# A sixth kept weight unit, norm weights applied at the split, and plain fp32 for the early linear units of a two-layer trunk

## The chip, the cores and the metric

One Trainium2 chip, one of its cores. The metric is the device time of one execution in microseconds (us). Engines: PE (TensorE) does matmuls, ACT (ScalarE) and DVE (VectorE) element-wise work, POOL (GpSimd) a few small operations, SP (SyncE) issues the DMAs.

## What is computed

256 tokens of width 2048 pass through two layers. Layer 0 mixes tokens with a state-space model and a gated linear unit, layer 1 with latent attention; each is followed by a feed-forward layer. Around every sub-layer stand two RMS norms, with weights `norm_g[l, 0..3]`:

```python
h = rmsnorm(x, norm_g[l, 0])
m = s5_mixer(h, ...)            # layer 0; layer 1: mla_mixer(h, ...)
x = x + rmsnorm(m, norm_g[l, 1])
h = rmsnorm(x, norm_g[l, 2])
f = conv_ffn(h, w_gate[l], w_up[l], conv_w[l], conv_b[l], w_down[l])
x = x + rmsnorm(f, norm_g[l, 3])
```

`s5_mixer` ends in `val, gate = split(gelu(y) @ w_glu + b_glu)` and `val * sigmoid(gate)`; `w_glu` is 2048 x 4096. All of it is fp32.

## The kernel before, in words

Tokens lie on the 128 partitions in two blocks (`tb` 0 and 1). A weight unit is 1 MB, loaded by `wunit` (L76) into `raw` (two buffers). `split` (L72) cuts it in two: ACT copies a rounded high part (L73, fp32r), DVE subtracts it and leaves the remainder (L74). `mm3` (L107) then multiplies with three fp32r matmuls: high by high, high by remainder, remainder by high. A `raw` buffer is free when both halves are split. The activations are kept as such pairs too, transposed, in the tiles `act`.

The state-space stage (`s5`) runs 18 turns; in turn n it works on pieces n, n-1 and n-2 of sixteen. Small loads `bc` and `g` for the next piece are issued by SP (L415, L417). After each fourth piece `part_d` (L545) splits a quarter of the mixer's output, and four early linear units (`glu_early`, L243) join the list `todo`; each turn takes at most one from it. They make the first two of four column blocks of the value and of the gate, one quarter of the contraction at a time. `glu_rest` (L624) does what is left, then column blocks 2 and 3.

At the end of each sub-layer block 0's last column block comes first, so that its norms run while PE works on block 1. For this the last units of weights are kept (`held`), split into tiles of their own (slots of `HOLD5` and `HOLD`, L36 and L38): five units in `glu_rest`, four in the feed-forward layers and in attention. Block 0 uses each unit as it comes, block 1 uses all of them afterwards.

The chain of one block is then: `finish` (linear stage only, L625), `finish_chunk` (L163: ACT squares the chunk and sums, DVE multiplies by the norm weight on L166), `post_norm` (L168: reciprocal root with one POOL power, then four times the residual sum on L172, the squares on ACT, and on L178 the product with the next norm's weight), `pre_scale` (L180: a second reciprocal root and, on L182, a diagonal tile `xh`), `pre_turn` (L185: PE multiplies by that diagonal and so transposes and scales, L191; four 512-column splits follow). `done(tb, 0)` calls all but the turn, `done(tb, 1)` the turn. Block 1's turn is called by the next layer as `tail()`, behind that layer's first products for block 0, for which it too keeps its first four units (L737 in `ffn`, L858 in `attention`). Only the feed-forward layers use L178; attention puts its norm weight into its own weights (L100).

The framework orders each engine's instructions by a plan made when the kernel is built, from program order and estimated times; the chip then runs every queue in that order. So the next layer's splits may stand between the links of a chain.

Of the kernel before, what the change touches and what calls it, by code (L numbers as in the profile page):

```python
# [15 lines left out]
P = 128  # L16
# [19 lines left out]
HOLD5 = ((0, 2), (4, 6), (10, 12), (8, None), (None, None))  # L36
LATE = ((1, 1), (2, 1), (3, 1), (2, 0), (3, 0))
# [7 lines left out]
def tile_trunk(ctx: ExitStack, tc: tile.TileContext, a: dict):  # L45
# [84 lines left out]
    def gain_tile(src):  # L130
        return T(env["ap"], [P, D], F32, "gb", 2), src
# [36 lines left out]
    def post_norm(f, fst, tb, x, xst, g):  # L168
        r = rstd1(fst[tb], D)
        for n in range(NCH):  # L170
# [6 lines left out]
            if g is not None:  # L177
                dve.tensor_tensor(f[tb][:, c], x[tb][:, c], g[0][:, c], op=ALU.mult)  # L178

    def pre_scale(xst):  # L180
        d = T(env["ap"], [P, 512], F32, "xh", 2)[:, :P]
        dve.tensor_scalar(d, ident, rstd1(xst, D), None, op0=ALU.mult)  # L182
        return d

    def pre_turn(h, d, tb):  # L185
        for n in range(NCH):
# [5 lines left out]
            split(*acts4(tb, n, slice(0, 4)), ptv)  # L192
# [49 lines left out]

    def glu_early(f, n, b, half):  # L243
        hv = glu_load(n, b, half)
        banks = [accb(), accb()]
        for tb in range(NB):
            hk, u = hv
            for i, (wh, wl) in enumerate(u):
                for k in range(hk):
                    j = i * hk + k  # L250
                    mm3(banks[tb], *acts(tb, 4 * b + j), wh[:, k, :], wl[:, k, :], j == 0, j == 3)
        o = half * 1024 + n * 512
# [8 lines left out]
    def s5(f):  # L261
        with tc.tile_pool(name="s5", bufs=2) as q1:
# [277 lines left out]
            def glu_steps(b):  # L540
                for n in range(2):
                    for half in range(2):
                        yield glu_early(f, n, b, half)

            def part_d(qt, yg):  # L545
                act_tiles()
                for hh in range(2):
# [7 lines left out]
                    for tb in range(NB):  # L555
                        hi, lo = acts4(tb, qt, slice(0, 4))
                        split(av(hi), av(lo), ptv.rearrange("p t (j c) -> p t j c", j=4)[:, :, :, 16 * tb : 16 * tb + 16])
# [19 lines left out]
            for n in range(nb + 2):  # L577
# [14 lines left out]
                if n >= 2 and m % PB == PB - 1:  # L592
                    part_d(m // PB, yg)
                    todo.append(glu_steps(m // PB))
# [8 lines left out]
    gkv, gq = T(cp, [P, KT], F32, "gkv"), T(cp, [P, KT], F32, "gq")  # L603
    sync.dma_start(gkv, a["gkv"])
# [19 lines left out]
    def glu_rest(q1, todo, f, fst, gains, done):  # L624
        def finish(n, tb, banks, bb):  # L625
# [7 lines left out]
            finish_chunk(f, fst, tb, n, gains[0])  # L633
# [12 lines left out]
        for n in range(2, 4):  # L646
            banks = [(wk if n % 2 == 0 else accb)() for _ in range(4)]
            held = []
            for b in range(4):
                for half in range(2):  # L650
                    if n == 3 and (b, half) > (1, 0):
                        late = LATE[len(held)]
                        held.append((*late, glu_load(n, *late, HOLD5[len(held)])))
# [5 lines left out]
                if n == 2 and b < 2:  # L659
                    if b == 0:  # L660
                        gain_load(gains[0])
# [5 lines left out]
                if n == 3 and b == 0:  # L667
# [3 lines left out]
                    gain_load(gains[1])  # L671
                    bb = bias(n)
            pb = banks
        for tb in range(NB):
# [4 lines left out]
            finish(3, tb, banks, bb)  # L679
# [4 lines left out]
    def ffn(l, tail, gains, f, fst, done):  # L684
        with tc.tile_pool(name=f"ff{l}", bufs=2) as q1:
# [42 lines left out]
            for part, npair in enumerate(PARTS):  # L728
                hid = []
                for pr in range(p0, p0 + npair):  # L730
                    banks = [wk(), wk()] if pr == 0 else [[wk(), wk()] for _ in range(2)]
                    held = []
                    for which, w in enumerate((wg, wu)):
                        for kh in range(2):
                            v = w[:, 8 * kh : 8 * kh + 8, pr * S : (pr + 1) * S]
                            if pr == 0:
                                held.append((which, kh, wunit(v, 8, S, slots=HOLD[len(held)])))  # L737
# [37 lines left out]
                if part == len(PARTS) - 2:  # L775
                    for g in gains:
                        if g is not None:
                            gain_load(g)
# [5 lines left out]
                def evac(n, tb, bank):  # L784
# [5 lines left out]
                    if last:  # L790
                        finish_chunk(f, fst, tb, n, gains[0])
# [26 lines left out]
    def attention(tail, gains, f, fst, done):  # L818
        with tc.tile_pool(name="at", bufs=2) as q1:
# [34 lines left out]
            for which, (w, gain) in enumerate(((wdkv, gkv), (wdq, gq))):  # L854
                banks = [accb(), accb()]
                held = []
                for un in range(4):
                    hv = wunit(  # L858
                        w[:, 4 * un : 4 * un + 4, 0:RANK], 4, RANK, gain[:, 4 * un : 4 * un + 4],
                        slots=(None, None) if which else HOLD[un],  # L860
                    )
# [158 lines left out]
            for g in gains:  # L1020
                gain_load(g)
            for n in range(NCH):
                banks = [accb(), accb()] if n else wob
                held = []
                for un in range(0 if n else 3, 4):
                    if n < NCH - 1:
# [4 lines left out]
                for tb in range(NB):  # L1031
                    if tb:
                        for un, hv in enumerate(held):
                            down(banks[1], un, 1, hv)
                        if held:
                            done(0, 1)
                    c = f[tb][:, n * 512 : (n + 1) * 512]
                    act.activation(c, banks[tb], AF.Copy)
# [140 lines left out]
```

## Time and profile before

| | us |
|---|---|
| median of 3 runs (2193.27 to 2194.26) | 2193.63 |
| the profiled execution | 2187.58 |
| its span in the profile | 2185.8 |
| PE busy in the span | 2079.0 (95%) |
| DVE busy | 1408.8 (64%) |
| ACT busy | 1122.4 (51%) |
| POOL busy | 19.8 (1%) |

Busy time of PE includes matmuls that overlap; what counts at a border is the idle time that a row shows in brackets, and what ended it. An fp32 matmul leaves two records, an fp32r matmul one.

### The profile page before, as it was taken

What the parts mean: (1) busy time and instruction counts of PE and PEld (TensorE: products, weight loads), DVE (VectorE), ACT (ScalarE), POOL (GpSimd) and SP (SyncE); (2) the same over time, 40 slices, a digit from 0 to 9 for tenths busy, and PEclk for the clock granted to TensorE, in tenths of its full rate; (3) what the DMA queues carried; (4) which work ended last, traced back from release to release, by engine and by line L of the source; (5) the groups of instructions that cost most, each with busy time, mean ns of one, the idle gap of its engine ahead of it and who ended that gap; (6) DMA issues with size and microseconds to landing.
All of it is one profiled execution on the core that took longest, in us unless ns stands there. A gap on an engine that the chain in (4) does not pass through costs nothing.

```text
span 2185.8 us, 32404 instructions
## 1 busy us (share of the span) xinstructions
PE 2079.0 (95%) x13268; PEld 1764.2 (81%) x13268; DVE 1408.8 (64%) x1940; ACT 1122.4 (51%) x1695; POOL 19.8 (1%) x57
## 2 busy tenths in 40 slices
PE   3788999899999999999989999989999999999998
PEld 2566777888888888888878998788888888888886
DVE  7999666666466556655686665566646655665567
ACT  6677445455455445544464554545545544554444
POOL 0000000000000000000000000000000000000000
PEclk9999999999999999999999999999999999999999
DMA  4132476455565555555564434635555555555654
GB/s 131 50 98 75 154 233 206 145 188 179 193 197 187 193 193 191 178 190 193 192 200 129 136 118 155 212 123 189 189 193 193 180 187 193 193 183 184 194 191 154
DMA packets 280966, 374.74 MB, mean 171 GB/s; under 512 B 9200, under 2 KB 196208, under 8 KB 279792
## 3 DMA queue, kind: packets, MB, share of 16 engines
q1 hardware_dynamic: 280816, 372.66, 52.4%
q8 instruction: 104, 1.70, 0.3%
q14 instruction: 46, 0.38, 0.1%
HBM read 370.54 MB, written 2.10 MB: 170 GB/s over the span
## 4 chain that ended last, share of the span: by engine, by line
PE 82%; DVE 10%; DMA 4%; ACT 3%; issue 1%; POOL 0%; SPq 0%; DVEq 0%; POOLq 0%; ACTq 0%
PE wk L114 29%; PE wk L115 15%; PE acc L108 9%; PE acc L109 9%; PE acc L110 9%; DMA raw<-in_w_glu 3%; PE wk L108 2%; PE wk L109 2%; PE wk L110 2%; DVE wlo L74 2%; PE acc L191 1%; DVE x L74 1%; ACT whi L73 1%; DVE f L431 1%; DVE f L430 1%
## 5 line engine op out<-in xcount | busy, mean ns | idle before, releaser
L74 DVE TENSOR_TENSOR wlo<-raw,whi 128x1024 fp32r<-128x1024 f32 (+2 forms) x640 | 761.0, 1191 | 584.0 <-ACT whi L73 579.3
L73 ACT ACTIVATE whi<-raw 128x1024 fp32r<-128x1024 f32 (+2 forms) x640 | 658.3, 1031 | 635.3 <-PE wk L114 245.6
L114 PE MATMUL wk<-act,whi 128*128 128x512 f32 x2688 | 941.9, 395 | 0.0
L115 PE MATMUL wk<-act,wlo 128*128 128x256 f32 x2688 | 753.0, 280 | 0.0
L114 PEld LDWEIGHTS wk<-act,whi 128*128 128x128 f32 x2688 | 504.1, 188 | 119.3
L115 PEld LDWEIGHTS wk<-act,wlo 128*128 128x128 f32 x2688 | 507.4, 189 | 0.3
L108 PE MATMUL acc<-whi,hh 128*128 128x512 f32 x652 | 255.4, 392 | 0.0
L109 PE MATMUL acc<-wlo,hh 128*128 128x512 f32 x652 | 255.3, 392 | 0.0
L110 PE MATMUL acc<-whi,hl 128*128 128x512 f32 x652 | 254.3, 391 | 0.0
L108 PEld LDWEIGHTS acc<-whi,hh 128*128 128x128 f32 x652 | 122.4, 188 | 27.2 <-ACT hh L73 0.5
L109 PEld LDWEIGHTS acc<-wlo,hh 128*128 128x128 f32 x652 | 122.4, 188 | 27.0 <-DVE wlo L74 0.5
L110 PEld LDWEIGHTS acc<-whi,hl 128*128 128x128 f32 x652 | 122.4, 188 | 26.9
L108 PE MATMUL acc<-whi,act 128*128 128x512 f32 (+1 forms) x332 | 126.4, 381 | 2.7 <-ACT act L73 2.7
L109 PE MATMUL acc<-wlo,act 128*128 128x512 f32 (+1 forms) x332 | 124.9, 377 | 1.9 <-DVE wlo L74 1.9
L110 PE MATMUL acc<-whi,act 128*128 128x512 f32 (+1 forms) x332 | 124.3, 375 | 0.1
L765 DVE SCALAR_TENSOR_TENSOR cv<-gs,cw,cv 128x255 f32<-128x255 f32 (+1 forms) x168 | 77.2, 480 | 3.0
L109 PEld LDWEIGHTS acc<-wlo,act 128*128 128x128 f32 x332 | 62.5, 188 | 14.9 <-DVE wlo L74 4.0
L108 PEld LDWEIGHTS acc<-whi,act 128*128 128x128 f32 x332 | 62.5, 188 | 14.5 <-ACT act L73 3.0
L110 PEld LDWEIGHTS acc<-whi,act 128*128 128x128 f32 x332 | 62.5, 188 | 11.5 <-DVE act L74 0.5
L763 ACT ACTIVATE cv<-gs,cb,cw 128x256 f32<-128x256 f32 x84 | 50.5, 601 | 36.5 <-DVE gs L715 36.5
L714 ACT ACTIVATE us<-wk 128x256 f32<-128x256 f32 x84 | 31.7, 380 | 60.3 <-PE wk L115 60.3
L714 ACT ACTIVATE gs<-wk 128x256 f32<-128x256 f32 x84 | 32.0, 381 | 59.8 <-PE wk L115 59.8
(282 smaller groups left out, 2342.5 us busy)
## 6 DMA issues: line engine op xcount, KB each, us to landing
raw<-in_w_gate SPq DMA_DIRECT2D x88, 1024.0 KB, 5.0
raw<-in_w_up SPq DMA_DIRECT2D x88, 1024.0 KB, 4.9
raw<-in_w_down SPq DMA_DIRECT2D x88, 1024.0 KB, 4.9
raw<-in_w_glu SPq DMA_DIRECT2D x32, 1024.0 KB, 6.2
raw<-in_w_o SPq DMA_DIRECT2D x16, 1024.0 KB, 4.9
raw<-in_w_ukv SPq DMA_DIRECT2D x8, 1024.0 KB, 5.3
gb<-in_norm_g SPq DMA_DIRECT2D x6, 1024.0 KB, 6.7
raw<-in_w_uq SPq DMA_DIRECT2D x8, 768.0 KB, 4.4
```

Of the source, the lines that this page charges most:

```text
L73: act.activation(hi, src, AF.Copy)
L74: (eng or dve).tensor_tensor(lo, src, hi.bitcast(F32), op=ALU.subtract)
L108: pe.matmul(o, lh, rh, start=first, stop=False)
L109: pe.matmul(o, lh, rl, start=False, stop=False)
L110: pe.matmul(o, ll, rh, start=False, stop=last)
L114: pe.matmul(ov, lh, r, start=first, stop=False)
L115: pe.matmul(ov[:, 0, :], ll, r[:, 0, :], start=False, stop=last)
L191: pe.matmul(ptv[:, k, :], h[:, o : o + P], d, start=True, stop=True)
L430: dve.tensor_tensor(f1, zt(0, 0, 9, 1), bc(2, 9), op=ALU.mult)
L714: act.activation(z[:, ft, :], two[ft][:, S:], AF.Copy)
L763: act.activation(cv[:, ft, :], gv[:, ft, :], AF.Identity, scale=cw[:, 2, n : n + 1], bias=cb[:, n : n + 1])
L765: dve.scalar_tensor_tensor(cv[:, ft, sh:], gv[:, ft, : S - sh], cw[:, 2 - sh, n : n + 1], cv[:, ft, sh:], op0=ALU.mult, op1=ALU.add,)
```

## The change

Three things, with what they need:

- `glu_rest` keeps six units instead of five. In attention the last unit of column block 2 is kept as well.
- L178 goes. `pre_turn` gets the norm's weight as a column per 128 channels (`gf`, loaded at the start) and splits 128 columns at a time, with the weight as a scale. One gain buffer `gb` goes, and its load.
- In three of four quarters the early linear units become `glu_full`: `part_d` copies the activations once more as plain fp32 (`ax`), and eight fp32 matmuls of 512 columns read `raw` itself, without a split.

In addition `behind` (`tc.issue_after`) puts DVE work behind block 0's L182 in DVE's queue: block 1's `finish` and L166, and the remainders of the next layer's kept units (units 1 to 3 in `ffn`, 2 and 3 in `attention`).

```diff
-HOLD5 = ((0, 2), (4, 6), (10, 12), (8, None), (None, None))
-LATE = ((1, 1), (2, 1), (3, 1), (2, 0), (3, 0))
+HOLD6 = ((0, 2), (4, 6), (10, 12), (14, 16), (8, None), (None, None))
+LATE = ((1, 1), (2, 1), (3, 1), (1, 0), (2, 0), (3, 0))
...
-        return T(env["ap"], [P, D], F32, "gb", 2), src
+        return T(env["ap"], [P, D], F32, "gb", 1), src
...
         sq_acc(c, fst[tb][:, n : n + 1])
-        dve.tensor_tensor(c, c, g[0][:, n * 512 : (n + 1) * 512], op=ALU.mult)
+        with behind(env["turn"] if tb else None):
+            dve.tensor_tensor(c, c, g[0][:, n * 512 : (n + 1) * 512], op=ALU.mult)
...
             sq_acc(x[tb][:, c], xst[:, n : n + 1])
-            if g is not None:
-                dve.tensor_tensor(f[tb][:, c], x[tb][:, c], g[0][:, c], op=ALU.mult)
...
+    def behind(ins):
+        return nullcontext() if ins is None else tc.issue_after(ins)
...
-    def pre_turn(h, d, tb):
+    def pre_turn(h, d, tb, g):
...
-            split(*acts4(tb, n, slice(0, 4)), ptv)
+            hi, lo = acts4(tb, n, slice(0, 4))
+            if g is None:
+                split(hi, lo, ptv)
+                continue
+            for k in range(4):
+                gk = g[:, 4 * n + k : 4 * n + k + 1]
+                act.activation(hi[:, k, :], ptv[:, k, :], AF.Copy, scale=gk)
+                dve.scalar_tensor_tensor(
+                    lo[:, k, :], ptv[:, k, :], gk, hi[:, k, :].bitcast(F32), op0=ALU.mult, op1=ALU.subtract
+                )
...
+    def glu_full(f, n, b, half, ax):
+        raw = T(env["wp"], [P, 4, 512], F32, "raw")
+        col = half * D + n * 512
+        sync.dma_start(raw, glu_w[b][:, :, col : col + 512])
+        banks = [accb(), accb()]
+        for tb in range(NB):
+            for j in range(4):
+                pe.matmul(banks[tb], ax[:, j, tb * P : (tb + 1) * P], raw[:, j, :], start=j == 0, stop=j == 3)
+        glu_keep(f, n, b, half, banks)
...
                 act_tiles()
+                ax = None if qt == 3 else T(q1, [P, 4, S], F32, "ax", 1)
...
+                        if ax is not None:
+                            act.activation(av(ax[:, :, tb * P : (tb + 1) * P]), src, AF.Copy)
...
+    for l in range(2):
+        sync.dma_start(gf[l], a["gf"][l])
     sync.dma_start(gkv, a["gkv"])
...
-                    if n == 3 and (b, half) > (1, 0):
+                    if n == 3 and (b, half) > (0, 1):
...
-                    gain_load(gains[1])
                     bb = bias(n)
...
-            finish(3, tb, banks, bb)
+            with behind(env["turn"] if tb else None):
+                finish(3, tb, banks, bb)
             done(tb, 0)
...
-                                held.append((which, kh, wunit(v, 8, S, slots=HOLD[len(held)])))
+                                with behind(before if held else None):
+                                    held.append((which, kh, wunit(v, 8, S, slots=HOLD[len(held)])))
...
+                    with behind(before if which == 0 and un > 1 else None):
+                        hv = wunit(
...
+                    if n == NCH - 2 and un == 3:
+                        late = (load(n, un, (10, 12)), banks)
+                        down(banks[0], un, 0, late[0])
+                        chunk(n, 0, banks)
...
+                    if tb and held:
+                        down(late[1][1], 3, 1, late[0])
+                        chunk(NCH - 2, 1, late[1])
                         for un, hv in enumerate(held):
                             down(banks[1], un, 1, hv)
+                        done(0, 1)
...
                 if not last:
-                    dg[tb] = pre_scale(xst[tb])
+                    dg[tb], ins = pre_scale(xst[tb])
+                    if tb == 0:
+                        env["turn"] = ins
             elif not last:
-                pre_turn((x if gn is None else f)[tb], dg[tb], tb)
+                pre_turn(x[tb], dg[tb], tb, gpre)
```

## Rows read from the trace of the kernel before

**Rows 1.** Stage windows: us; busy PE, PEld, DVE, ACT, POOL; clock, DMA share, GB/s.

```profile
98.00:245.00 147.00, 128.64 (x2050) 98.16 (x2043) 131.04 (x206) 107.88 (x201) 0.25 (x4) 1.00 0.26 75
...
262.00:313.00 51.00, 46.75 (x191) 36.14 (x190) 37.48 (x51) 24.21 (x31) 0.00 (x0) 0.97 0.82 263
```

**Rows 2.** Timeline of PE, first border: start us, us, line, tiles, [idle before].

```profile
385.56 0.39 PE L110 MATMUL acc<-whi,act 128*128 128x512 f32 x1
...
393.24 6.28 PE L191 MATMUL acc<-xh,f 128*128 128x128 f32 x32 [7.29 <-DVE xh L182]
...
410.76 3.73 PE L191 MATMUL acc<-xh,f 128*128 128x128 f32 x32
```

**Rows 3.** Windows at the first border, columns as in rows 1.

```profile
390.00:400.00 10.00, 6.76 (x38) 6.76 (x39) 9.78 (x20) 4.64 (x11) 2.28 (x3) 0.58 0.70 243
```

**Rows 4.** Timeline of DVE, first border, columns as in rows 2.

```profile
375.60 0.69 DVE L631 TENSOR_TENSOR f<-acc,bias 128x512 f32<-128x512 f32 x1 [1.75 <-PE acc L110]
...
384.77 1.29 DVE L178 TENSOR_TENSOR f<-x,gb 128x512 f32<-128x512 f32 x2
...
389.17 1.22 DVE L74 TENSOR_TENSOR x<-raw,x 128x1024 fp32r<-128x1024 f32 x1
...
392.90 0.28 DVE L182 TENSOR_SCALAR xh<-cst,rs_r 128x128 f32<-128x128 f32 x1
...
404.12 0.15 DVE L145 TENSOR_REDUCE tot<-st 128x1 f32<-128x5 f32 x1
...
405.39 0.29 DVE L182 TENSOR_SCALAR xh<-cst,rs_r 128x128 f32<-128x128 f32 x1
```

**Rows 5.** Timeline of POOL, first border.

```profile
380.04 0.55 POOL L147 TENSOR_TENSOR rs_y<-tot,cst 128x1 f32<-128x1 f32 x1 [273.01 <-DVE tot L145]
...
389.33 1.45 POOL L147 TENSOR_TENSOR rs_y<-tot,cst 128x1 f32<-128x1 f32 x1 [8.70 <-DVE tot L145]
```

**Rows 6.** Timelines of ACT, DVE and PE, attention to feed-forward layer.

```profile
1414.44 0.58 ACT L1038 ACTIVATE f<-acc 128x512 f32<-128x512 f32 x1
...
1417.82 1.41 DVE L172 SCALAR_TENSOR_TENSOR x<-f,rs_r,x 128x512 f32<-128x512 f32 x2
...
1428.87 5.61 PE L191 MATMUL acc<-xh,f 128*128 128x128 f32 x32 [7.41 <-DVE xh L182]
...
1445.75 3.73 PE L191 MATMUL acc<-xh,f 128*128 128x128 f32 x32
```

**Rows 7.** Timelines of DVE, ACT and PE, feed-forward layer to attention.

```profile
1138.05 2.73 DVE L172 SCALAR_TENSOR_TENSOR x<-f,rs_r,x 128x512 f32<-128x512 f32 x4
...
1144.40 0.69 DVE L166 TENSOR_TENSOR f<-f,gb 128x512 f32<-128x512 f32 x1
...
1141.69 0.19 ACT L139 ACTIVATION_READ_ACCUMULATOR junk<-x 128x1 f32 x1
...
1145.34 5.72 PE L191 MATMUL acc<-xh,x 128*128 128x128 f32 x32 [5.92 <-DVE xh L182]
```

**Rows 8.** Timeline of PE: first and last of 24 matmuls of an early linear unit.

```profile
186.47 0.58 PE L108 MATMUL acc<-whi,act 128*128 128x512 f32 x1
...
191.92 0.39 PE L110 MATMUL acc<-whi,act 128*128 128x512 f32 x1
```

**Rows 9.** Groups of ACT, 98 to 245 us: busy us, mean ns | idle before, releaser.

```profile
L489 ACT ACTIVATE vs<-wk 128x128 f32<-128x128 f32 x11 | 3.1, 283 | 0.0
...
L420 ACT ACTIVATE bc<-bc,cst 128x128 f32<-128x128 f32 x8 | 3.2, 397 | 3.9 <-DMA bc<-in_sBC 3.9
```

**Rows 10.** Groups of DVE, 98 to 245 us, columns as in rows 9.

```profile
L74 DVE TENSOR_TENSOR wlo<-raw,whi 128x1024 fp32r<-128x1024 f32 x18 | 21.9, 1220 | 6.1 <-ACT whi L73 6.1
```

**Rows 11.** Groups of PE, 98 to 245 us, columns as in rows 9.

```profile
L108 PE MATMUL acc<-whi,act 128*128 128x512 f32 x72 | 29.7, 412 | 2.7 <-ACT act L73 2.7
...
L497 PE MATMUL wk<-cst,vs 128*128 128x128 f32 x21 | 6.0, 299 | 6.1 <-ACT vs L488 6.1
```

**Rows 12.** Timeline of SP's queue at the start.

```profile
0.74 0.38 SPq L604 DMA_DIRECT2D gkv<-in_gkv  x1
```

More of the change, by code (lines that the diff above doesn't have):

```diff
@@ L1 @@
 import math
-from contextlib import ExitStack
+from contextlib import ExitStack, nullcontext
 import concourse.bass as bass
@@ L603, in tile_trunk @@
     gkv, gq = T(cp, [P, KT], F32, "gkv"), T(cp, [P, KT], F32, "gq")
+    gf = [T(cp, [P, KT], F32, f"gf{l}") for l in range(2)]
+    for l in range(2):
+        sync.dma_start(gf[l], a["gf"][l])
     sync.dma_start(gkv, a["gkv"])
@@ L622, in rope_tables, with glu_rest @@
         sincos(rsin, rcos, rr, rn, cst[:, C_RS : C_RS + 1])
-    def glu_rest(q1, todo, f, fst, gains, done):
+    def glu_rest(q1, todo, f, fst, gain, done):
         def finish(n, tb, banks, bb):
@@ L632, in finish @@
             dve.tensor_tensor(c, c, sg, op=ALU.mult)
-            finish_chunk(f, fst, tb, n, gains[0])
+            finish_chunk(f, fst, tb, n, gain)
         def bias(n):
@@ L660, in glu_rest @@
                     if b == 0:
-                        gain_load(gains[0])
+                        gain_load(gain)
                     bb = bias(b)
@@ L678, in glu_rest, with ffn @@
                 done(0, 1)
-            finish(3, tb, banks, bb)
+            with behind(env["turn"] if tb else None):
+                finish(3, tb, banks, bb)
             done(tb, 0)
         return lambda: done(1, 1)
-    def ffn(l, tail, gains, f, fst, done):
+    def ffn(l, tail, before, gain, f, fst, done):
         with tc.tile_pool(name=f"ff{l}", bufs=2) as q1:
@@ L775, in ffn @@
                 if part == len(PARTS) - 2:
-                    for g in gains:
-                        if g is not None:
-                            gain_load(g)
+                    gain_load(gain)
                 def load(n, un, slots=(None, None)):
@@ L790, in evac @@
                     if last:
-                        finish_chunk(f, fst, tb, n, gains[0])
+                        finish_chunk(f, fst, tb, n, gain)
                 if last:
@@ L815, in ffn, with attention @@
         return lambda: done(1, 1)
-    def attention(tail, gains, f, fst, done):
+    def attention(tail, before, gpost, f, fst, done):
         with tc.tile_pool(name="at", bufs=2) as q1:
@@ L1018, in attention, with chunk @@
                     q = {"kv": kv, "qn": qn, "qr": rope(q1, qs_, br[:, S:])}
-            for g in gains:
-                gain_load(g)
+            gain_load(gpost)
+            env["yp"] = q1
+            def chunk(n, tb, banks):
+                c = f[tb][:, n * 512 : (n + 1) * 512]
+                act.activation(c, banks[tb], AF.Copy)
+                finish_chunk(f, fst, tb, n, gpost)
             for n in range(NCH):
@@ L1030, in attention @@
                         down(banks[0], un, 0, held[un])
-                for tb in range(NB):
-                    if tb:
+                for tb in range(NB if n == NCH - 2 else 0, NB):
+                    if tb and held:
+                        down(late[1][1], 3, 1, late[0])
+                        chunk(NCH - 2, 1, late[1])
                         for un, hv in enumerate(held):
                             down(banks[1], un, 1, hv)
[L1035 to L1038, printed above, removed]
-                    finish_chunk(f, fst, tb, n, gains[0])
+                        done(0, 1)
+                    chunk(n, tb, banks)
                     if held:
@@ L1146, in _arrays @@
         "b_glu": g("ssm_b_glu"),
+        "gf": np.stack([pn(g("norm_g")[l, 2]) for l in range(2)]),
         "gkv": pn(g("kv_norm_g")),
```

44 lines of the change are left out of this document (23 added, 21 removed).

## The prediction

> **What bounds the kernel now.** I read the page's 40 slices first: PE is nearly full from slice 5 on, except at the layer borders and in the first eighth. The stages come next. In the state-space stage (98 to 245 us, nine early linear units) DVE is busy 131.0 of 147.0 us and PE 128.6, so DVE is the fullest and PE has 18.4 us of gaps; in the dense linear stage after it PE misses 4.3 of 51 us [rows 1]. At a border the chain of waits leaves PE for DVE. At the first one PE ends the held work of block 1 at 385.9 and starts block 0's turn at 393.24, held up by xh (the diagonal that `pre_scale` makes on L182); the turn itself takes 6.28 us, while the same turn for block 1 takes 3.73 [rows 2], because the granted clock is 0.58 of full there, a mix of 2.4 and 1.2 GHz after PE's pause [rows 3]. So a border costs a pause and a slow turn.
>
> **What xh waits for.** At the first border the last product of block 0 is taken at 375.60 and xh begins at 392.90: 17.3 us [rows 4]. In between DVE also issues weight remainders of the next layer (six of L74, the one at 389.17 stands for them), block 1's finish and two pairs of L178 products, each pair 1.29 us [rows 4]; POOL's power takes 0.55 us while little runs and 1.45 beside them [rows 5]. At the attention border it is 14.4 us from the copy of the last product (1414.44) to PE's restart (1428.87), with PE idle 7.41 [rows 6].
>
> A clean chain is put together from three pieces that were disturbed little. From the copy of the last product to the first L172 is 3.4 us (1414.44 to 1417.82) [rows 6]. Four L172 with the squares behind them, without L178, last 3.85 (1138.05 to 1141.9) [rows 7]. From the reduce to the end of xh is 1.6 (404.12 to 405.68) [rows 4]. Sum 8.9; I take 9.2 with hand-overs.
>
> **The change, part by part.**
>
> First border (`glu_rest` to the first feed-forward layer). Block 1's finish and the DVE remainders of the next layer's units 1 to 3 go behind xh, and L178 goes. The chain then ends near 375.6 + 9.2 = 384.8. PE has work of block 1 until 385.9 [rows 2]. The sixth kept unit moves 12 matmuls of 0.23 us = 2.7 us from before to after block 0's end [rows 8]; part of it will be run early, while block 0's last loads are awaited, so I take the turn's start at 386.5 (385.9 to 388.6) instead of 393.24: 6.7 us. Without the pause the turn runs at the full clock: 6.28 - 3.73 = 2.5 us. Against this, DVE must do all that was put off before block 1's turn. That turn's xh now stands at 405.39, 5.4 us ahead of PE at 410.76 [rows 2, 4]; the second time moves up by about 9 us, and DVE sheds eight L178 (5.2 us at 0.65) but gains small remainders, so it may be late by 0 to 2 us. I take 8.5 us gained; bounds 3 (the gap returns at block 1) and 11.
>
> The weights at the split. Per block four 512-column splits become sixteen of 128 columns. ACT takes 0.283 us for a 128x128 tile out of PSUM [rows 9] and DVE 0.28 for a 128x128 product, xh itself [rows 4]: 16 x 0.28 = 4.5 us against 4 x 0.65 = 2.6, so 1.9 us more per block and engine. It hides behind the 3.7 us of the turn and the matmuls behind it, which take the sixteen pieces in order; without that cover it is 1.9 us for each of four turns. From below it can't be a gain beyond L178, counted above. I take 0, and keep 0 to 2 us per border. The Trainium skill's page "VectorE: DVE Perf Modes", section "The TRN2 errata", says that each instruction pays a fixed extra time, so tiles should hold 512 elements or more; by its table (120 cycles plus one per column from PSUM at 0.96 GHz) sixteen small ones would cost an estimated 4.1 us against 2.6, so 1.5 more per block. The rows make it 1.9, so the rule stands here, and either figure is hidden by the same turn.
>
> Attention to the second feed-forward layer. Same edits, and one unit of column block 2 is kept as well. The chain would end at 1414.4 + 9.2 = 1423.6, with PE idle from 1421.4; the turn began at 1428.87 and took 5.61 [rows 6]. Gain 5.2 for the pause and 1.9 for the clock (5.61 - 3.73): I take 7.3, as the kept unit can fill the rest; bounds 2 and 9.5.
>
> First feed-forward layer to attention. Here only units 2 and 3 of the next layer are put behind xh, and block 1's L166. The remainders in the chain belong to units 0 and 1; two L166 (the one at 1144.40 and one like it) stand between the reduce and xh [rows 7]. Gain 0.7, bounds -1 and 2; most of the pause (5.92) stays [rows 7].
>
> Early linear units in plain fp32. Twelve units drop two ACT splits and two DVE remainders each: 18 remainders in the stretch, 21.9 us of DVE, and 6.1 us of waiting before them [rows 10]. PE pays. The 24 matmuls of a unit ran from 186.47 to 191.92, 0.23 each, so 5.5 us [rows 8]. The new unit has 8 fp32 matmuls of 512 columns. The nearest row is the turn, sixteen fp32 matmuls of 128 columns in 3.73 us [rows 2], 0.22 apiece, so 0.89 for 512 and 7.1 per unit: 1.5 us more. Nine units make 13.5 us, and PE's 128.6 becomes 142.1 of 147, while DVE falls to 109: PE becomes the bound. The stretch shrinks by at most 4.9 and, if every gap stays, grows by 13.5. The gaps that were waits for splits go (L108's 2.7), and most of L497's 6.1, where ACT had splits ahead of vs [rows 11]; with some of the rest I take 12 of 18.4, so +1.5. The three other units add up to 4.5 where PE is dense, and the split-free start returns some 2.4 (two remainders, 1.22 each [rows 10]) and part of the gaps behind it. Together I take +1; bounds -8 and +17.
>
> Two more loads head SP's queue (the new `gf`), each like gkv, 0.38 us [rows 12]: 0 to +0.8, as all first loads queue behind them; I take +0.5. The broadcast of the second norm weight goes (1 MB, in the dense stage, whose PE gaps are 4.3 us [rows 1]): 0 to -4, I take -1.5, since linear weights can be fetched earlier. With one gain buffer the next gain waits for the last L166 of block 1; its use is a whole layer later, so 0 unless SP stands still on it: 0 to 2.
>
> **Sum.** -8.5 - 7.3 - 0.7 + 1 + 0.5 - 1.5 = -16.5 us, on the profiled execution's own 2187.58 us (span 2185.8): 2171.1. The three timed runs have the median 2193.63, 6.05 above it, so 2177.1 for the median.
>
> **Rivals.**
>
> PE isn't the bound in the state-space stage. The Trainium skill's page "Perfetto Trace Analysis", section "Identifying the Most-Contended Engine", says to take the engine with the highest occupancy and relieve it. As a mechanism here: DVE, the fullest [rows 1], loses 21.9 us and the stretch shortens by it, giving 2177 - 1 - 22 = 2154. For it: DVE is busy in 89% of the stretch. Against it: PE has only 18.4 us of gaps for 13.5 us of new work. Chance 0.13.
>
> The pauses move on to block 1. The work put off on DVE isn't done when PE reaches block 1's turn, and half of the borders' 15.8 us comes back: 2185. For it: DVE is busy 9.78 of 10 us at the border [rows 3]. Chance 0.20. The same time results if the kept units do nothing, their block 1 work being run early in waits for loads.
>
> Slower: SP stands still. A raw buffer was free after the splits; now it is free after the unit's last fp32 matmul. If the next raw load stands ahead of the small bc loads in SP's queue, each of nine turns of the stage waits. ACT's L420 already waits 3.9 us in eight turns for bc [rows 9]. The price is up to 7.1 - 2.4 = 4.7 us per turn; at 3 us it is 27 us, giving 2204. It decides from 1.8 us per turn on, where it eats the 16.5. Against it: the planner sees the later release and can order bc first. Chance 0.07.
>
> **Numbers.** My forecast has 0.60, with its own range of 2168 to 2186. The range over all cases is 2161 to 2190: it takes in the halved borders and most of the way to the DVE rival, and leaves out SP. A change of 0.2% (4.4 us) is about what can be told from none. Faster: 0.58 of the forecast, 0.13 and 0.14 of the halved borders, 0.85; same 0.08; slower 0.07.
>
> **What would show it.** Right: at the first and third border the turn of block 0 starts within 3 us of PE's last held matmul, its 32 records take about 3.7 us, and no L178 exists; the pause at the second border stays above 4 us; in the state-space stage PE is busier than DVE and the stage ends within 8 us of before; fp32 units take about 7 us. Wrong: a new pause ahead of block 1's turn, a stage that is 15 us shorter or longer, or ACT waiting for bc for several us per turn.

## The result and the profile after

| | before | changed |
|---|---|---|
| median, us (14 runs each, same chip) | 2195.35 (2190.70 to 2202.53) | 2200.86 (2197.69 to 2205.82) |
| ratio, 95% interval | 1 | 1.0027 [1.0016, 1.0038] |
| profiled execution, its span | 2187.58, 2185.8 | 2198.68, 2196.9 |
| PE, DVE, ACT busy | 2079.0, 1408.8, 1122.4 | 2097.6, 1382.1, 1106.4 |

The change makes the kernel slower by 5.5 us (the interval allows 3.5 to 8.3); 2177 with a range of 2161 to 2190 was predicted. The borders (the places where one sub-layer hands over to the next) did gain, and the state-space stage lost more.

The windows of rows 1 for the changed kernel, and its three quarters by themselves (columns as there):

```profile
98.00:245.00 147.00, 132.40 (x1860) 80.88 (x1868) 106.97 (x178) 80.94 (x175) 0.25 (x4) 0.98 0.26 74
262.00:313.00 51.00, 46.01 (x211) 30.45 (x210) 28.80 (x38) 17.35 (x22) 0.00 (x0) 1.00 0.74 228
96.00:162.00 66.00, 58.48 (x757) 34.34 (x754) 49.19 (x88) 39.68 (x85) 0.25 (x4) 0.97 0.30 85
162.00:220.00 58.00, 51.87 (x764) 32.08 (x763) 46.90 (x73) 32.80 (x72) 0.00 (x0) 1.00 0.25 72
220.00:266.00 46.00, 43.58 (x532) 25.93 (x531) 19.61 (x38) 13.35 (x32) 0.00 (x0) 0.96 0.20 55
```

DVE fell from 131.0 to 107.0 us of 147 [rows 1] and PE rose to 132.4: PE is now the fuller engine, and the stage is longer. The groups of the changed kernel, 98 to 256 us, that answer to rows 9 to 11 (PE, DVE, ACT; columns as there):

```profile
L261 PE MATMUL acc<-raw,ax 128*128 128x512 f32 x145 | 65.4, 604 | 1.4 <-ACT ax L584 1.4
L491 PE MATMUL acc<-K,cst 64*32 64x256 f32 x640 | 19.6, 379 | 5.3 <-DVE K L476 5.2
L521 PE MATMUL wk<-cst,vs 128*128 128x128 f32 x22 | 6.5, 308 | 6.2 <-DVE act L74 3.5 <-ACT vs L512 2.5
...
L454 DVE TENSOR_TENSOR f<-z,bc 128x1152 f32<-128x1152 f32 x9 | 12.2, 1357 | 16.3 <-PE wk L423 16.3
L282 DVE TENSOR_TENSOR f<-acc,f 128x512 f32<-128x512 f32 x10 | 6.9, 690 | 16.1 <-PE acc L261 16.0
...
L584 ACT ACTIVATE ax<-wk 128x256 f32<-128x256 f32 x12 | 7.9, 661 | 7.2 <-PE acc L261 7.2
L444 ACT ACTIVATE bc<-bc,cst 128x128 f32<-128x128 f32 x7 | 2.8, 402 | 8.6 <-DMA bc<-in_sBC 8.6
```

The lines of before that answer to L491, L454 and L282 (groups of PE and DVE, 98 to 256 us):

```profile
L467 PE MATMUL acc<-K,cst 64*32 64x256 f32 x640 | 19.6, 379 | 1.4 <-DVE K L452 1.1
...
L430 DVE TENSOR_TENSOR f<-z,bc 128x1152 f32<-128x1152 f32 x9 | 12.1, 1349 | 0.0
...
L258 DVE TENSOR_TENSOR f<-acc,f 128x512 f32<-128x512 f32 x12 | 8.2, 684 | 1.9 <-PE acc L110 1.9
```

DVE, which had been the fullest, now waits 16 us for PE in each of two lines, where it waited 0.0 and 1.9. L521 (L497 in rows 11) still waits 6.2 us in all, but the part of it that ends with ACT's vs fell from 6.1 to 2.5; 3.5 are now a wait for DVE's remainders of `act`. ACT has twelve new copies, 7.9 us. What a wait looks like, in the timeline of PE and DVE:

```profile
146.28 7.03 PE L261 MATMUL acc<-raw,ax 128*128 128x512 f32 x16
...
153.24 0.65 PE L423 MATMUL wk<-ET,U 128*32 128x128 f32 x16
...
155.04 1.36 DVE L454 TENSOR_TENSOR f<-z,bc 128x1152 f32<-128x1152 f32 x1 [3.43 <-PE wk L423]
```

One fp32 unit takes 7.0 us (7.1 was predicted). PE runs its queue in order, so the state-space matmuls of L423 stand behind all of it. The last of them read an older one of the three buffers of the tile that L454 writes (`f1`), and DVE stands idle until they have done so.

The borders, in the timeline of PE (answers to rows 2, 6 and 7; the first is the last matmul ahead of the turn):

```profile
403.70 0.39 PE L110 MATMUL acc<-whi,act 128*128 128x512 f32 x1
404.09 3.84 PE L193 MATMUL acc<-xh,x 128*128 128x128 f32 x32
409.98 0.39 PE L108 MATMUL acc<-x,act 128*128 128x256 f32 x1 [2.05 <-DVE act L201]
...
423.12 3.84 PE L193 MATMUL acc<-xh,x 128*128 128x128 f32 x32 [1.46 <-DVE xh L181]
...
1159.55 5.83 PE L193 MATMUL acc<-xh,x 128*128 128x128 f32 x32 [4.90 <-DVE xh L181]
...
1437.12 3.84 PE L193 MATMUL acc<-xh,x 128*128 128x128 f32 x32 [0.91 <-DVE xh L181]
1442.48 0.39 PE L108 MATMUL acc<-x,act 128*128 128x256 f32 x1 [1.52 <-DVE act L201]
1455.89 3.84 PE L193 MATMUL acc<-xh,x 128*128 128x128 f32 x32 [1.74 <-DVE xh L181]
```

Block 0's turn (the transposes by `xh`) follows the held work without a pause at the first border and takes 3.84 us in place of 6.28 [rows 2]; at the third the pause falls from 7.41 [rows 6] to 0.91. The clock there, which was 0.58 [rows 3], is full (window, columns as in rows 1):

```profile
402.00:412.00 10.00, 7.95 (x59) 7.06 (x58) 8.94 (x24) 8.10 (x22) 0.54 (x1) 1.00 0.24 70
```

But there are new pauses behind the turn (2.05 and 1.52) and ahead of block 1's (1.46 and 1.74), which had none. DVE at the first border shows where they come from:

```profile
393.27 0.69 DVE L662 TENSOR_TENSOR f<-acc,bias 128x512 f32<-128x512 f32 x1 [1.75 <-PE acc L110]
...
403.75 0.29 DVE L181 TENSOR_SCALAR xh<-cst,rs_r 128x128 f32<-128x128 f32 x1
403.95 0.68 DVE L660 TENSOR_TENSOR sg<-acc,bias 128x512 f32<-128x512 f32 x1
404.55 1.21 DVE L74 TENSOR_TENSOR x<-raw,x 128x1024 fp32r<-128x1024 f32 x1
...
408.80 2.69 DVE L201 SCALAR_TENSOR_TENSOR act<-acc,gf,act 128x128 fp32r<-128x128 f32 x10
...
412.52 0.15 DVE L145 TENSOR_REDUCE tot<-st 128x1 f32<-128x5 f32 x1
412.59 1.22 DVE L74 TENSOR_TENSOR x<-raw,x 128x1024 fp32r<-128x1024 f32 x1
...
416.51 1.22 DVE L74 TENSOR_TENSOR wlo<-raw,whi 128x1024 fp32r<-128x1024 f32 x1
...
422.77 0.29 DVE L181 TENSOR_SCALAR xh<-cst,rs_r 128x128 f32<-128x128 f32 x1
```

Block 0's chain is down from 17.3 [rows 4] to 10.5 us (393.27 to 403.75; 9.2 was estimated, with the 0.3 of xh itself, and two weight remainders still stand in it). Behind xh stands what was put off (L660, L74 and their like), between the pieces L201 that PE waits for. From block 1's reduce (412.52) to its xh are 10.25 us, against 6.4 for block 0's (397.35 to 403.75): four weight remainders stand in it.

### The profile page after: what moved, and what is told of

Same layout as the page of the kernel before. It is cut to its first block, busy times and chain, and to the rows that moved or that the text cites. A ratio compares the mean times of both kernels' runs of the same rounds, so it can differ in the third digit from the quotient of the medians.

```text
span 2196.9 us, 32219 instructions
## 1 busy us (share of the span) xinstructions
PE 2097.6 (95%) x13172; PEld 1745.5 (79%) x13172; DVE 1382.1 (63%) x1948; ACT 1106.4 (50%) x1723; POOL 18.5 (1%) x57
## 4 chain that ended last, share of the span: by engine, by line
PE 82%; DVE 9%; ACT 3%; DMA 3%; issue 1%; POOL 0%; SPq 0%; DVEq 0%; POOLq 0%; ACTq 0%
PE wk L114 28%; PE wk L115 15%; PE acc L109 9%; PE acc L108 9%; PE acc L110 9%; PE acc L261 3%; DMA raw<-in_w_glu 2%; PE wk L108 2%; PE wk L109 2%; PE wk L110 2%; DVE wlo L74 1%; PE wk L423 1%; ACT junk L139 1%; DVE f L455 1%; ACT whi L73 1%
## 5 line engine op out<-in xcount | busy, mean ns | idle before, releaser
L74 DVE TENSOR_TENSOR wlo<-raw,whi 128x1024 fp32r<-128x1024 f32 (+1 forms) x612 | 726.8, 1190 | 567.6 <-ACT whi L73 564.9
L73 ACT ACTIVATE whi<-raw 128x1024 fp32r<-128x1024 f32 (+1 forms) x612 | 628.4, 1030 | 615.7 <-PE wk L114 246.6
L261 PE MATMUL acc<-raw,ax 128*128 128x512 f32 x192 | 86.1, 602 | 1.4 <-ACT ax L584 1.4
L109 PE MATMUL acc<-wlo,act 128*128 128x512 f32 (+1 forms) x220 | 81.3, 370 | 2.4 <-DVE wlo L74 2.4
L108 PE MATMUL acc<-whi,act 128*128 128x512 f32 (+1 forms) x220 | 80.5, 369 | 1.8 <-ACT whi L73 1.8
L110 PE MATMUL acc<-whi,act 128*128 128x512 f32 (+1 forms) x220 | 80.5, 366 | 0.0
L261 PEld LDWEIGHTS acc<-raw,ax 128*128 128x128 f32 x192 | 36.7, 193 | 42.8 <-issue 40.7
L74 DVE TENSOR_TENSOR x<-raw,x 128x1024 fp32r<-128x1024 f32 x36 | 43.4, 1221 | 29.1 <-ACT x L73 29.0
```

The lines of the kernel that those rows point to most:

```text
L73: act.activation(hi, src, AF.Copy)
L74: (eng or dve).tensor_tensor(lo, src, hi.bitcast(F32), op=ALU.subtract)
L108: pe.matmul(o, lh, rh, start=first, stop=False)
L109: pe.matmul(o, lh, rl, start=False, stop=False)
L110: pe.matmul(o, ll, rh, start=False, stop=last)
L261: pe.matmul(banks[tb], ax[:, j, tb * P : (tb + 1) * P], raw[:, j, :], start=j == 0, stop=j == 3)
```

## The experiments

Theory A after the result: the fp32 units cost 14 to 18 us, because PE is the bound of the state-space stage once it does them, and the rest of the change gains 7 to 13. Rival B: the fp32 units are near zero, as predicted, and something else in the change cost the time. Ratios are against the kernel before on the same chip, whose median was 2195.0 to 2196.3; the runs lie on four chips, so ratios and not medians are compared between them. A ratio is turned into us by 2195.

**Before, traced again.** No edit.

> The kernel before, unchanged, for a second profile. The profiled execution of before (2187.58) lies 6 us under the median of its runs and all comparisons of traces go against it. Theory A (run to run variation lies in the dense stretches and at the start): the second column block starts within 2 us of 289.4, the borders' pauses stay within 1 us of 7.45, 6.1 and 7.6 and the span differs by 3 to 10 us over the rest. Theory B (the first profile's state-space stage was itself a lucky run): the block starts 4 us later or more, and the fp32 units' cost against it is overstated by as much.

One run: 2197.53 us, span 2195.7. In PE's timeline the last quarter's transposes, the start of column block 2 (which ends the state-space stage and its early units), and the two turns at the first border:

```profile
256.23 1.03 PE L550 MATMUL wk<-cst,yg 128*128 128x128 f32 x8
...
293.97 0.39 PE L108 MATMUL wk<-whi,act 128*128 128x512 f32 x1
...
398.41 6.37 PE L191 MATMUL acc<-xh,f 128*128 128x128 f32 x32 [7.12 <-DVE xh L182]
...
416.04 3.73 PE L191 MATMUL acc<-xh,f 128*128 128x128 f32 x32
```

Theory B of this run holds in part: block 2 starts 4.5 us later than the 289.43 of the first trace, so that trace overstates what the stage lost. The borders' pauses (7.12, 6.56 and 7.04) are as they were. This trace, 1.2 us above the median of 2196.29 taken beside it, is what the others are held against from here.

**Without fp32 units, and fp32 units alone.**

```diff
-                ax = None if qt == 3 else T(q1, [P, 4, S], F32, "ax", 1)
+                ax = None
```

The second kernel is the one before with `glu_full`, `ax` and the calls for it, and nothing else of the change.

> The changed kernel with all early linear units split as before (no fp32 units, no ax). Theory A (the fp32 units' extra 1.4 us of PE each are exposed, because PE takes over as the bound of the state-space stage): 14 to 18 us below the changed kernel, so 7 to 13 us below the kernel before, ratio to it 0.994 to 0.997; the turn of block 0 at the first border starts 14 to 18 us earlier than in the changed kernel's trace. Theory B (the stage grew through the new loads at the start and another plan, not through fp32): within 4 us of the changed kernel.

> The kernel before with the fp32 early linear units alone. Theory A: 12 to 18 us above the kernel before, ratio 1.0055 to 1.008, and column block 2 of the linear stage starts 14 to 18 us later. Theory B: within 4 us of the kernel before.

Without them: 2186.16, ratio 0.9952 [0.9935, 0.9969]. Alone: 2208.47, ratio 1.0051 [1.0033, 1.0069]. The rest of the change is a gain of 10.5 us and the fp32 units are a loss of 11 (alone) to 16 us (in the change). Theory A holds in size, B falls; what the loss is made of is taken apart below. Two of A's marks were missed: alone the units cost a little less than its 12 to 18 us, and block 0's first turn starts 12.3 us earlier without them (391.80 against 404.09), not 14 to 18. Without fp32 units column block 2 starts at 294.00, as in the second trace of before; with them at 305.94 (changed) and 304.94 (alone).

**The order on DVE, and the sixth unit.** The first two kernels are without fp32 units. In the first `behind` does nothing; the second has the five entries of `HOLD5` and `LATE` again, and attention keeps no unit of column block 2; the third is the kernel before with the order alone (`behind` and its four calls), L178 and the five units.

```diff
     def behind(ins):
-        return nullcontext() if ins is None else tc.issue_after(ins)
+        return nullcontext()
...
-LATE = ((1, 1), (2, 1), (3, 1), (1, 0), (2, 0), (3, 0))
+LATE = ((1, 1), (2, 1), (3, 1), (2, 0), (3, 0))
```

> As no_fp32, and without the DVE order (behind does nothing). Theory C (the pinned DVE order carries the borders' gain): 5 to 12 us above no_fp32, pauses of over 4 us ahead of block 0's turns at the first and third border. Rival D (the gain comes from L178's removal and the sixth kept unit; the planner would order well by itself): within 2 us of no_fp32, pauses under 3 us.

> As no_fp32, with five kept units in the linear stage and four in attention, as before the change. If the sixth unit is what covers the chain: 3 to 6 us above no_fp32, with PE pauses of 2 to 3 us ahead of block 0's turns at the first and third border. If block 1's work of that unit is run early anyway, in waits for loads: within 2 us of no_fp32.

> The kernel before with the DVE order alone (block 1's finish and L166 and the next layer's kept remainders behind block 0's L182); L178, five kept units and split units stay. Theory C (the order alone carries the gain; norm weights at the split and the sixth unit return nothing): 6 to 10 us below the kernel before, within 3 us of no_fp32. Rival E (order and L178's removal are both needed): 0 to 4 us below the kernel before, with pauses of 3 to 5 us left ahead of block 0's turns, since L178 stands in the chain.

Without the order: 2195.90, 1.0001 [0.9991, 1.0011]: all 10 us of the rest's gain are gone. With five units: 2187.25, 0.9955 [0.9939, 0.9972]: the sixth unit gives nothing that can be told. Pauses did come back ahead of block 0's turns (0.60 at the first border, 3.76 in place of 0.91 at the third), but block 1's turn, which had waited 1.48 and 1.79 there, then follows without one. The order alone: 2191.34, 0.9990 [0.9979, 1.0000], some 2 us, as rival E had it. The first border of the kernel without the order, then of the one with the order alone (PE):

```profile
398.59 6.20 PE L193 MATMUL acc<-xh,x 128*128 128x128 f32 x32 [6.54 <-DVE tot L145]
```

```profile
395.29 3.84 PE L195 MATMUL acc<-xh,f 128*128 128x128 f32 x32 [2.42 <-DVE xh L183]
...
411.92 0.58 PE L109 MATMUL acc<-wlo,act 128*128 128x256 f32 x1 [2.63 <-DVE wlo L74]
```

Without the order, the removal of L178 and the sixth unit leave the pause nearly as it was (7.12 in the second trace of before). With the order alone the pause falls to 2.42 (3.49 at the third border), and the work put off comes back as a wait for remainders. Order and removal of L178 together give the gain, with five units as with six.

**The small splits.** The first kernel leaves the norm weights out and splits 512 columns at a time; the second does a bank's four ACT pieces and then its four DVE pieces; the third is the second with one more attention unit behind xh. All are without fp32 units.

```diff
-            if g is None:
+            if True:
                 split(hi, lo, ptv)
                 continue
...
             for k in range(4):
                 gk = g[:, 4 * n + k : 4 * n + k + 1]
                 act.activation(hi[:, k, :], ptv[:, k, :], AF.Copy, scale=gk)
+            for k in range(4):
+                gk = g[:, 4 * n + k : 4 * n + k + 1]
                 dve.scalar_tensor_tensor(
...
-                    with behind(before if which == 0 and un > 1 else None):
+                    with behind(before if which == 0 and un > 0 else None):
```

> As no_fp32, with the second norm's weights left out of the computation and one split of 512 columns per chunk. Theory F (sixteen small splits, in which ACT and DVE take turns on one PSUM bank, make the pauses of 2.2 and 1.7 us behind block 0's turns): both pauses under 0.6 us, 3 to 6 us below no_fp32. Rival G (the pauses come from the work that was put off on DVE and stands ahead of the splits): pauses of over 1.2 us stay, within 2 us of no_fp32.

> As no_fp32, but with the four ACT pieces of a chunk in program order ahead of its four DVE pieces. Theory F, if the turns between ACT and DVE make the pauses: pauses behind block 0's turns under 1.5 us, 1 to 4 us below no_fp32. Rival G: within 1.5 us of no_fp32, pauses as there.

> The version with split units and with the turn's pieces grouped by engine (2185.10), with one more of attention's kept units put behind the turn's scaling (units 1, 2 and 3 in place of 2 and 3). Theory A (the pause of 4.94 us ahead of attention's first turn is VectorE's weight work that is still ahead of the chain): that pause falls by 2 to 4 us, the time by 1 to 3 us, 2182 to 2184. Theory B (the work put off comes back between the two blocks' turns): the first pause falls, one of the same size stands ahead of block 1's turn or in the next unit, 2184 to 2187.

2183.17 (0.9952 [0.9940, 0.9965]), 2185.10 (0.9962 [0.9950, 0.9975]) and 2186.48 (0.9959 [0.9947, 0.9971]): none can be told from 2186.16. The first border with grouped pieces, then the second with one more unit behind (PE):

```profile
389.00 3.84 PE L193 MATMUL acc<-xh,x 128*128 128x128 f32 x32
393.60 0.36 PE L108 MATMUL acc<-x,act 128*128 128x256 f32 x1 [0.76 <-DVE act L203]
...
409.45 5.46 PE L193 MATMUL acc<-xh,x 128*128 128x128 f32 x32 [3.54 <-DVE xh L181]
```

```profile
1144.39 5.18 PE L193 MATMUL acc<-xh,x 128*128 128x128 f32 x32 [3.56 <-DVE xh L181]
```

The first border without the small splits (PE):

```profile
396.76 0.39 PE L108 MATMUL acc<-x,act 128*128 128x256 f32 x1 [0.23 <-DVE act L74]
...
410.85 5.28 PE L193 MATMUL acc<-xh,x 128*128 128x128 f32 x32 [2.41 <-issue]
```

Without the small splits the pause behind the turn all but goes (2.05 to 0.23), as theory F had it, but not the time: one of 2.41 stands ahead of block 1's turn, which then takes 5.28. With grouped pieces the pause behind the turn falls to 0.76 and the one ahead of block 1's turn grows to 3.54. With one more unit behind, the second border's pause falls from 4.77 to 3.56, less than theory A's 2 to 4, and nothing of it is seen in the time, as theory B has it. DVE has the same work between two turns; what is taken from one pause turns up in the next.

**Why the fp32 units cost so much.** Five kernels: three of the twelve units in fp32; all split, but the copies `ax` still written; all twelve in fp32 without the copies (the units then read the rounded high part of the activations and leave their remainder out); and, for the last two, the units' loads in the ring of the split halves, with and without copies.

```diff
-                        yield glu_early(f, n, b, half) if ax is None else glu_full(f, n, b, half, ax)
+                        yield glu_early(f, n, b, half) if ax is None or (n, half) != (0, 0) else glu_full(f, n, b, half, ax)
...
+                        yield glu_early(f, n, b, half)
...
-                pe.matmul(banks[tb], ax[:, j, tb * P : (tb + 1) * P], raw[:, j, :], start=j == 0, stop=j == 3)
+                pe.matmul(banks[tb], A[b][:, j, 0, tb * P : (tb + 1) * P].bitcast(F32), raw[:, j, :], start=j == 0, stop=j == 3)
...
-        raw = T(env["wp"], [P, 4, 512], F32, "raw")
+        raw = [T(wp, [P, 2, 512], F32R, w, nb).bitcast(F32) for w in ("whi", "wlo")]
```

> As no_fp32, with one early linear unit of each of the first three quarters in plain fp32 (three units instead of none or twelve). Theory A (PE bound, each fp32 unit's extra 1.4 us exposed): 2 to 5 us above no_fp32. Rival H (PE takes over only when many units are fp32; the first ones relieve DVE): 0 to 7 us below no_fp32.

> All early linear units are split as before, but ScalarE still writes the fp32 copies of the activations of the first three quarters (12 copies of about 0.66 us, 7.9 us in all) and their three tiles stand in memory; nothing reads them. Three fp32 units cost 9.7 us (2195.87 against 2186.16), where three units' extra TensorE time, 3 x 1.4 us, gives 4.2. Theory A (only the matmuls cost, and the order of the units around them): the copies are hidden, 2185 to 2188, and the second column block starts 4 to 5 us after the last quarter's end as without fp32. Theory B (the copies, ahead of ScalarE's splits and keeps at each quarter's end, hold the state-space stage up by themselves): 2190 to 2195, the second column block starts 3 to 8 us later than the 294 us of the version without fp32.

> The twelve fp32 units stay, but read the high part of the split activations in place of a copy: no copies on ScalarE, and the remainder of the activations is left out of these units. Everything else is the changed kernel (2200.86). Theory A (the twelve units' longer TensorE time costs by itself): within 3 us of the changed kernel, 2198 to 2203. Theory B (the copies and the wait for them carry a large part): 2190 to 2195.

> The changed kernel (2200.86), but the twelve fp32 units load into the ring of the split halves (whi and wlo, three of each, empty in those quarters) in place of the two raw tiles, in two transfers of half the size; copies, sums and order are unchanged. In the changed kernel an fp32 unit holds its raw tile until TensorE has used it, so the first split unit of the last quarter has its load issued only at 272.6 us and TensorE pauses 3.2 us in all behind the last fp32 unit; with the copies left out the same handover cost about 10 us. Theory A (this hold is a part of the fp32 units' cost): the second column block starts 3 to 5 us earlier than the changed kernel's 305.9, the time is 2195 to 2198. Theory B (TensorE's own longer time is all of it; what the handover gives is lost again): no earlier than 304.5, the time 2199 to 2202.

> As the run with fp32 units in the split halves' ring, and the units read the high part of the activations in place of a copy (the remainder is left out of these twelve units, and no copies are written). From the four traces the three quarters cost 12.9 us more than without fp32 units, 7.1 more with fp32 and no copies, 4.6 more with copies and no fp32, and the handover 3.9 and 9.8. Theory A (three separate terms: matmuls, copies, handover): with copies and handover both gone the second column block starts at about 294 + 7.1 - 5 = 296 to 299, the time is 2188 to 2193. Theory B (whatever is taken away, another wait of the same size takes its place, as when the copies alone were left out): it starts at 303 to 306, 2197 to 2202.

The times, and three marks in PE's timelines: the transposes at the end of the first and of the last quarter (with the us between them), and the start of column block 2.

| kernel | median | ratio | first quarter's end | last quarter's end | between | column block 2 |
|---|---|---|---|---|---|---|
| before, second trace | 2196.29 | 1 | 98.85 | 256.23 | 157.4 | 293.97 |
| no fp32 | 2186.16 | 0.9952 | 99.42 | 257.46 | 158.0 | 294.00 |
| copies only | 2191.66 | 0.9976 [0.9963, 0.9990] | 100.6 | 263.3 | 162.7 | 297.99 |
| own ring, no copies | 2193.24 | 0.9985 [0.9975, 0.9995] | 93.33 | 260.49 | 167.2 | 298.22 |
| own ring | 2197.41 | 1.0009 [1.0001, 1.0018] | 94.34 | 263.75 | 169.4 | 301.11 |
| no copies | 2201.92 | 1.0026 [1.0015, 1.0036] | 94.4 | 259.61 | 165.2 | 305.92 |
| changed | 2200.86 | 1.0027 | 94.49 | 265.52 | 171.0 | 305.94 |
| one in four | 2195.87 | 1.0003 [0.9991, 1.0014] | 97.1 | 265.2 | 168.0 | 300.00 |

How steady the marks are, nine traces tell in which all early units are split (two of before, no fp32 and the six of the two sections above): column block 2 starts between 289.43 and 295.18, the time between the quarters' ends is 157.4 to 158.9, and from the last of them to column block 2 it is 35.1 to 38.5. So a step at column block 2 can be off by some 3 us.

From no fp32 to own ring without copies, to own ring and to the changed kernel, one thing is added at each step: the fp32 units in place of split ones 4.2 us at column block 2 (7.2 by the ratios), the copies 2.9 (5.3), the hold on `raw` 4.8 (4.0). The last step also takes away the room for a third unit loaded ahead (six half tiles against two whole ones), which wasn't tried apart from the hold. Both runs with the own ring came out as their theory A said (the second 0.2 us above its upper end). The copies without an fp32 unit that reads them cost the same 5.3 us by the ratios (4.6 between the quarters' ends), as theory B of that run had it. The run without copies alone went by its theory A, and for another reason than that theory gave: the copies' part was freed (the last quarter ends 5.9 us earlier) and lost to the hold. Rows of that kernel behind the last fp32 unit, from the timelines of PE, SP and ACT:

```profile
260.48 13.04 PE L261 MATMUL acc<-raw,act 128*128 128x512 f32 x30
277.88 0.86 PE L108 MATMUL acc<-whi,act 128*128 128x512 f32 x2 [4.36 <-ACT whi L73]
...
266.69 0.38 SPq L79 DMA_DIRECT2D raw<-in_w_glu  x1
...
276.77 2.00 ACT L73 ACTIVATE whi<-raw 128x1024 fp32r<-128x1024 f32 x2 [14.04 <-DMA raw<-in_w_glu]
```

The first split unit of the last quarter can be loaded only when an fp32 unit has been used up and gives back its `raw`, here at 266.69; PE is out of work at 273.5 and waits 4.36. In the changed kernel the load is issued at 272.60 and PE waits 1.21, 0.53 and 1.46. With the ring of the halves, `raw` is free from the start, and the same loads stand in SP's timeline right behind those of the inputs:

```profile
32.85 2.64 SPq L79 DMA_DIRECT2D raw<-in_w_glu  x2
```

One unit in four came out above both theories: 9.7 us more than without fp32 by the medians, 11 by the ratios, where A had 2 to 5. The copies' 5.3 are in it. The hold isn't seen there: PE waits for no weights between the quarters' ends, and from the last of them to column block 2 it is 34.8 us, as with copies only (34.7). Between the ends the trace is 5.4 us longer than with copies only, and PE is busy 9.3 us more (149.4 against 140.1), though three units bring some 4.5. With the rest goes a lower granted clock, 0.95 in that stretch against 0.99, which wasn't tried apart: the first of the three units, behind a pause for its copies, took 8.83 us in place of 7.03 at a clock of 0.81 (103 to 112 us).

```profile
103.01 8.83 PE L261 MATMUL acc<-raw,ax 128*128 128x512 f32 x16 [2.90 <-ACT ax L584]
```

## Why the prediction was wrong

Against the second trace of before, stretch by stretch:

| stretch | predicted | changed | without fp32 |
|---|---|---|---|
| start to column block 2 | 0 (+1 + 0.5 - 1.5) | +12.0 | 0.0 |
| to block 1's turn, first border | -8.5 | -4.9 | -5.2 |
| to block 1's turn ahead of attention | -0.7 | -1.1 | -1.1 |
| to block 1's turn, second feed-forward layer | -7.3 | -4.3 | -4.0 |
| to the last matmul | 0 | -0.4 | +0.1 |

The changed kernel's stretches add up to +1.3. The medians say 5.5; the difference is that this trace of before lies 2.2 us above the median of 2195.35 and the changed kernel's 2.2 below its own. Without fp32 units the start to column block 2 is unchanged, so the +0.5 for two more loads and the -1.5 for the broadcast that went add up to nothing that can be told; no run takes them apart.

**The step that failed: "I take 12 of 18.4" of PE's gaps.** The unit's price was right (7.0 us, some 17 us more PE time for twelve; the prediction's 0.22 a matmul is from start to start, by the 3.73 of its row it would be 0.23). That the gaps would swallow most of it was not. With copies and hold both gone, the stretch between the first and the last quarter's end is 167.2 us against 157.4 (windows of the second trace of before and of own ring without copies, columns as in rows 1):

```profile
98.85:256.23 157.38, 138.90 (x2153) 106.22 (x2146) 139.29 (x221) 111.45 (x205) 0.25 (x4) 1.00 0.27 78
```

```profile
93.33:260.49 167.16, 153.50 (x2065) 92.05 (x2064) 118.03 (x200) 83.68 (x177) 0.25 (x4) 0.99 0.24 72
```

Ten units lie in it, and PE is busy 14.6 us longer. The stretch grew by 9.8, so PE's gaps fell from 18.5 to 13.7: 4.8 us of them went, not 12. They weren't free room: in each turn PE, DVE and ACT hand on to each other, and while a unit stands on PE for 7 us the next link starts later. DVE's wait in L454 was not there before and is 16.3 in the changed kernel; PE's for K went up to 5.3. Of L521's 6.1 "most" was to go: ACT's part did shrink to 2.5, and a wait for DVE took its place. The growth of 9.8 lies nearer the bound from above, that every gap stays, than the 1.5 that was taken.

**Two terms were missing.** The twelve copies weren't costed at all: 7.9 us of ACT, 3 to 5 on the path. The hold on `raw` was seen, but only as the slower rival, SP standing still ahead of the bc loads. ACT's wait for bc did rise, from 3.9 [rows 9], which lay in two of the eight turns, to 8.6 in seven of seven; the profile puts no wait of another engine down to it. The hold was paid elsewhere, where the fp32 units hand over to split ones: from the last quarter's end to column block 2 it is 40.4 us in the changed kernel and 46.3 without copies, against 35.1 to 38.5 in the nine traces. On the other side the first quarter ended 4.4 us earlier, as the start is free of splits (2.4 and part of the gaps was predicted).

**The borders: right in mechanism, half in size.** The pause went and the turn runs at the full clock, 3.84 us, as forecast. The rival of the pauses that move to block 1 took the other half: pauses of 2.05 and 1.46 at the first border, 1.52 and 1.74 at the third. The 0 to 2 us kept for DVE's lateness ahead of block 1 was right in size there; of the 0 to 2 kept for the splits 0 was taken, and the traces show 2.05 and 1.52 behind the turn: "it hides behind the turn" overlooked that put-off remainders stand between the pieces. The cover of the sixth unit was over-valued: five do as well.

**Second border:** -0.7 against -1.1, with the pause above 4 us, as predicted.

Two rules. The Trainium skill's page "Perfetto Trace Analysis", section "Identifying the Most-Contended Engine", tells to optimize the engine with the highest occupancy first, and this change does so in the state-space stage. The traces disagree here: DVE shed 24 us of 147 and the stage ended 12 later, since the work moved to an engine that was 128.6 us busy itself. The Trainium skill's page "VectorE: DVE Perf Modes", section "The TRN2 errata", asks for 512 elements or more per instruction. The rows agree that small pieces are dear (ten L201 of 128 columns in 2.69 us, 0.27 each; four L74 of 512 without the small splits in 2.48), and the runs add that it was not on the path: 512-column splits gave no time that can be told.

What stays open: why the clock falls more often in the one-in-four run, and what else fills the difference between the marks at column block 2 (12.0) and the ratios (16.5) for the fp32 units; the intervals of the two ratios alone allow 6 us of it, and the spread of the mark 3. That more buffers of `f1` would let DVE run on past an fp32 unit follows from the wait of L454 and wasn't tried.

The version without fp32 units (2186.16, 0.9952) beats both kernels.

## What to carry to other kernels

An idle share of an engine is not room: where engines hand on to each other within a turn, a longer block of work on one delays the next link, and most of its extra time can be the price (9.8 of 14.6 us here). When work is moved between engines, list everything that comes with it (copies, and how long each input buffer is now held), and look where the old way begins again, for there the held buffer is missed. And put off no more work behind a critical chain than the time up to the next chain holds; the removal of work from the chain and the order that uses it were worth little apart here.

## What had not been expected

Two executions of the same program reached column block 2 at 289.43 and 293.97 us, with pauses at the borders that differ by 0.6 at most: a difference of one trace to another of 4.5 us up to that mark is no sign of a change. Twelve copies of 0.66 us that nobody reads cost 5 us. And three fp32 units of twelve cost, with the twelve's copies, 10 of the twelve's 15 us by the medians.
